# Early products with U in full single precision, more of them, and more gathered rows ahead of the dense stage

## The chip, the cores and the metric

One program on one core of one Trainium2 chip. The metric is the device time of one launch in microseconds (us); the time before is the median of three runs.

## The reference, cut to what matters

The program computes one layer for 512 prompt tokens and 32 sample tokens: retention, sparse attention, a gated sum of both, a layer norm, then PEER (product-key experts) and a last layer norm. The change lies in PEER:

```python
def block(xb):
    q = (xb @ wq).reshape(T, PEER_HEADS, PEER_DKEY).astype(jnp.float32)
    s1 = jnp.einsum('thd,hnd->thn', q[..., :half], subkeys[:, 0].astype(jnp.float32))
    s2 = jnp.einsum('thd,hnd->thn', q[..., half:], subkeys[:, 1].astype(jnp.float32))
    v1, i1 = lax.top_k(s1, PEER_TOPK)
    v2, i2 = lax.top_k(s2, PEER_TOPK)
    ...
    sc, sel = lax.top_k(cand, PEER_TOPK)
    eidx = jnp.take_along_axis(cidx, sel, axis=-1)
    g = jax.nn.softmax(sc, axis=-1)
    act = jax.nn.gelu(jnp.einsum('td,thkd->thk', xb.astype(jnp.float32), u[eidx].astype(jnp.float32)), approximate=False)
    return jnp.einsum('thk,thkd->td', g * act, v[eidx].astype(jnp.float32)).astype(x.dtype)
```

There are 16384 experts, each a row of U and a row of V of 1024 numbers; every token takes 16 of them for each of 8 heads.

## The kernel before, in words

PEER is done in two ways. For three tiles of 128 prompt tokens (DENSE, tiles 1 to 3) the kernel computes the products with **all** experts on TensorE and multiplies by gates that are zero for the experts not chosen. U and V come in 128 pieces of 128 experts (512 KB each). For the first prompt tile and the sample tokens (GATHER, tiles 0 and 4) it fetches the chosen rows one by one: a step fetches, for all 128 tokens of a tile, one row of U or V each (`rows`, L1303, an indirect DMA that GpSimd issues), and VectorE makes the dot product (L1316, `junk`) or adds the scaled row (L1322, `acc`). There are 320 such steps; they run anywhere after the choice of the gathered tiles.

The order of the program from the first layer norm on:

1. `first_norm` (L1061): normed rows are turned by TensorE and kept as two float32r parts, `x1h` and `x1l`.
2. `keys` (L1083): queries on TensorE, the 16 best keys on VectorE.
3. `choose` for GATHER (L1187, VectorE) beside `embedding` (L1139, TensorE).
4. `choose` for DENSE (L1187, VectorE): ends with `pick`, the chosen keys and gates.
5. `gate_tables` (L1259): 48 steps of 8 tokens. GpSimd makes `o2` (L1273), VectorE `o1` (L1275) and `o2` (L1277), both named `o` in the profile, TensorE multiplies them (L1282), ScalarE copies the result (L1283), which goes to DRAM as `gd`. Its first instruction on TensorE turns `pick` (L1264).
6. The dense stage (L1506): for each piece j, `u_phase(j)` (L1442) makes the activations of 384 tokens (product with U, gelu), and four pieces later `v_parts` and `v_product` (L1467, L1481) multiply by the gates and add the product with V into six PSUM tiles.
7. The last layer norms.

A product in float32r goes three times over the array (`mm3`, L157), because each operand is split in a high and a low part. The split of a weight piece (`weights`, L149, with `split`, L125) is a copy on ScalarE (`wh`, L126) and a subtraction (`wl`, L127) on VectorE, or on GpSimd. A piece of U takes 8 x 3 matmuls of 384 columns, a piece of V 6 x 3 of 512 columns.

Stages 1 to 5 are **filled** with work of the dense stage and with gathered rows. `u_early` (L938) makes the product of the next piece of U ahead of time. Before the gate tables its result goes to DRAM (`early`, `act_d`) and comes back in the dense stage (`gl`, L1448, then a gelu, L1449); the first KEPT ones made in the gate tables stay in SBUF (`kept`). `tick` (L953) decides: each step of a stage states what it costs TensorE, VectorE and ScalarE, and pieces are added until TensorE's account is as full as the others'. Rows are added in proportion to TensorE's account (RATE). The accounts are constants of the program (CF for `choose`, GY for `gate_tables`):

```python
while fill["pe"] < max(fill["dve"], fill["act"]) and fill["u"] < EARLY:
    u_early()
    fill["pe"] += 3.9
    fill["dve"] += 1.1 if UPOOL == 1 else 0.0
    fill["act"] += 1.4
```

EARLY is only a ceiling. As the program is built, 45 pieces are made early before (25 through DRAM, 20 kept), and 83 stay in the dense stage; 74 of the 320 row steps come ahead of it. With UPOOL = 2 the split of every other early piece is done by GpSimd.

Of the kernel before, what the change touches and what calls it, by code (L numbers as in the profile page):

```python
# [20 lines left out]
NT = 544  # L21
# [20 lines left out]
KEPT = 22  # L42
VR = 3
EARLY = 72
UPOOL = 2
# [4 lines left out]
CF = 0.85  # L50
# [9 lines left out]
GY = (1.8, 2.3, 1.2)  # L60
# [18 lines left out]
def tile_hybrid_step(ctx: ExitStack, tc: tile.TileContext, io):  # L79
# [24 lines left out]
    def moments(pieces, p0, p1, name):  # L104
        """1/sqrt(var + EPS) and -mean/sqrt(var + EPS) of the rows of [p, <= 512] views; the root by Newton's steps."""
# [23 lines left out]
    # ---------------------------------------------------------------- pools of the front  # L129
# [19 lines left out]
    def weights(src, n=1024, eng=V, raw=None, keep=None):  # L149
        """A [128, n] piece of a weight as its two float32r parts."""  # L150
# [26 lines left out]
    def project(chunk, evac):  # L177
        """Columns of a 128-wide chunk of W_in, transposed: [128, tokens]."""
# [8 lines left out]
    def project_nat(pieces, width, hook=lambda u: None, part=None):  # L187
        """Columns of W_in as they come: five tiles [128 tokens, columns]; pieces: (source, number of k), for width
        columns after the other. part: a tile for the sample group's four sums, each in 32 columns of the array (four
        k a piece); the fifth tile is then that group's alone."""  # L190
# [31 lines left out]
    def gates(n, tile_of):  # L222
        """Gates of the branches: the next chunks, as tanh(x / 2), to DRAM."""
# [6 lines left out]
    # ---------------------------------------------------------------- attention keys, indexer  # L230
# [29 lines left out]
    # places of the pages  # L260
# [17 lines left out]
    for i, t0 in enumerate(TILES):  # L278
# [3 lines left out]
        # keys of the attention, rotated  # L282
# [12 lines left out]
        # indexer keys: layer norm, rotated  # L295
# [43 lines left out]
    def rope_swap(dst, raw, cs, sn, blk, u, eng):  # L339
        """Rotation of rows in a chunk whose heads are blocks of 2*blk rows; sn has the source rows' signs."""  # L340
# [11 lines left out]
    # ---------------------------------------------------------------- queries of the attention  # L352
# [20 lines left out]
    # ---------------------------------------------------------------- indexer of the prompt  # L373
# [37 lines left out]
    # ---------------------------------------------------------------- indexer of the sample group  # L411
    # rows 32 q + 4 b + t: the q-th quarter of the past of token t of sequence b, then (q = 3) the new keys
# [64 lines left out]
    # the TOPK-th largest of each row, bit by bit; y = +-x so that it is not negative  # L477
# [453 lines left out]
    def u_dots(h, l):  # L931
        p = pst()
        for k in range(8):
            ks = slice(k * 128, (k + 1) * 128)
            mm3(p[:, :DT], h[:, ks], l[:, ks], x1h[:, k, D0:D0 + DT], x1l[:, k, D0:D0 + DT], k == 0, k == 7)
# [729 lines left out]
```

## Time and profile before

| | |
|---|---|
| median of 3 runs | 2661.93 us (2655.82 to 2664.12) |
| span of the profiled execution | 2726.3 us; the page gives no time of that execution besides its span |
| TensorE busy | 2478.5 us, 91% |
| VectorE busy | 1934.1 us, 71% |
| ScalarE, GpSimd busy | 35%, 36% |
| HBM traffic | 205 GB/s over the span |

Shares over the whole span mix stages with different limits, so the stages have to be looked at one by one. Names in the profile: PE is TensorE, PEld its weight loads, DVE VectorE, ACT ScalarE, POOL GpSimd. Starts of matmuls are measured, their ends are modelled and overlap the next start, so the tempo of matmuls is read from start to start. A matmul of two float32 operands is recorded twice. A granted clock of 1.00 is 2.4 GHz, the lower level is 1.2 GHz; what stands between is a mean over time at both.

### The profile page before, as it was taken

The numbers are of one execution on the slowest core, as the hardware profiler recorded it, in microseconds if no ns is written. First come the engines' busy times: TensorE is split into PE (matmuls) and PEld (weight loads), VectorE is DVE, ScalarE is ACT, GpSimd is POOL, SyncE is SP. The second block draws the span as 40 slices with busy tenths as digits, with TensorE's granted clock in tenths as the row PEclk, the third lists the DMA queues.
The fourth block names the chain that finished last, engine by engine and source line by source line (L and its number), as shares of the span: only waits on it lengthen the run. The fifth ranks groups of instructions, "written<-read, shape, count | busy, mean of one in ns | idle before, by whom it ended". The sixth has DMA issues, their size and how long they took to land.

```text
span 2726.3 us, 40425 instructions
## 1 busy us (share of the span) xinstructions
PE 2478.5 (91%) x15162; PEld 2164.6 (79%) x15162; DVE 1934.1 (71%) x3867; ACT 953.4 (35%) x1657; POOL 993.5 (36%) x773
## 2 busy tenths in 40 slices
PE   8789999999988999999887777789999999999996
PEld 8768988888655569889777766778988988888885
DVE  6685667755322245578999999977777877877777
ACT  3232333333232333243222354543333333333332
POOL 4530000001134412110356778833444444443442
PEclk9889999999998999999998998899999999999998
DMA  6322243545675554232256566579888888998883
GB/s 204 106 85 92 71 167 113 195 127 191 226 227 156 152 173 160 96 138 72 93 184 203 201 224 223 206 259 349 294 317 310 315 321 306 332 319 308 300 314 126
DMA packets 233013, 562.71 MB, mean 206 GB/s; under 512 B 26576, under 2 KB 96400, under 8 KB 230896
## 3 DMA queue, kind: packets, MB, share of 16 engines
q1 hardware_dynamic: 140576, 287.83, 31.2%
q0 software_dynamic: 58368, 205.55, 21.6%
q10 hardware_dynamic: 33872, 66.73, 6.6%
q8 instruction: 119, 1.95, 0.3%
q14 instruction: 78, 0.64, 0.1%
HBM read 491.08 MB, written 68.95 MB: 205 GB/s over the span
## 4 chain that ended last, share of the span: by engine, by line
PE 65%; DVE 19%; issue 5%; DMA 4%; another core or an unknown queue 2%; ACT 2%; POOL 1%; SPq 0%; ACTq 0%; DVEq 0%; POOLq 0%
PE ps L160 7%; PE ps L158 7%; PE ps L159 7%; PE po L159 6%; PE po L158 6%; PE po L160 6%; PE act L158 4%; PE act L159 4%; PE act L160 4%; DVE o L1277 2%; DVE junk L1316 2%; PE nat L158 2%; PE nat L160 2%; DVE acc L1322 2%
## 5 line engine op out<-in xcount | busy, mean ns | idle before, releaser
L126 ACT ACTIVATE wh<-wraw 128x1024 fp32r<-128x1024 f32 (+2 forms) x265 | 278.7, 1052 | 606.3 <-PE ps L159 207.8
L127 DVE TENSOR_TENSOR wl<-wraw,wh 128x1024 fp32r<-128x1024 f32 (+2 forms) x239 | 306.0, 1280 | 172.7 <-ACT wh L126 150.1
L1303 POOL DMA_INDIRECT rows<-u_rows,eidx x160 | 240.3, 1502 | 317.8 <-DVE junk L1316 254.4
L1303 POOL DMA_INDIRECT rows<-v_rows,eidx x160 | 240.9, 1505 | 278.9 <-DVE acc L1322 192.5
L159 PE MATMUL po<-vl,ah 128*128 128x512 f32 x768 | 301.5, 393 | 6.6 <-DVE vl L127 6.6
L158 PE MATMUL po<-vh,ah 128*128 128x512 f32 x768 | 299.7, 392 | 1.1 <-ACT vh L126 1.1
L160 PE MATMUL po<-vh,al 128*128 128x512 f32 x768 | 300.1, 391 | 0.0
L158 PE MATMUL ps<-xh,wh 128*128 128x272 f32 x960 | 284.6, 296 | 9.3 <-issue 7.7
L159 PE MATMUL ps<-xl,wh 128*128 128x272 f32 x960 | 281.8, 294 | 8.1 <-issue 8.1
L160 PE MATMUL ps<-xh,wl 128*128 128x272 f32 x960 | 283.1, 295 | 5.9 <-issue 5.9
L160 PE MATMUL ps<-x1h,wl 128*128 128x384 f32 (+1 forms) x616 | 205.2, 333 | 28.4 <-DVE wl L127 16.8
L1322 DVE SCALAR_TENSOR_TENSOR acc<-rows,co,acc 128x1024 f32<-128x1024 f32 x160 | 227.1, 1420 | 4.4 <-DMA rows<-v_rows,eidx 3.8
L158 PE MATMUL act<-x1h,wh 128*128 128x384 f32 x664 | 225.2, 339 | 1.3 <-ACT gl L1456 1.3
L159 PE MATMUL act<-x1l,wh 128*128 128x384 f32 x664 | 223.3, 336 | 0.0
L160 PE MATMUL act<-x1h,wl 128*128 128x384 f32 x664 | 223.2, 336 | 0.0
L1316 DVE SCALAR_TENSOR_TENSOR junk<-rows,x1n 128x1024 bf16<-128x1024 f32 x160 | 212.7, 1329 | 5.8 <-DMA rows<-u_rows,eidx 5.3
L158 PE MATMUL ps<-x1h,wh 128*128 128x384 f32 (+1 forms) x616 | 206.4, 335 | 11.0 <-ACT pph L1179 8.0
L159 PE MATMUL ps<-x1l,wh 128*128 128x384 f32 (+1 forms) x616 | 202.7, 329 | 0.3 <-DVE x1l L1081 0.3
L158 PEld LDWEIGHTS ps<-xh,wh 128*128 128x128 f32 x960 | 185.6, 193 | 21.2 <-issue 13.9
L821 POOL DMA_INDIRECT kv<-ckv,idp x128 | 123.3, 963 | 211.2 <-PE nat L862 153.7
L159 PEld LDWEIGHTS ps<-xl,wh 128*128 128x128 f32 x960 | 185.8, 194 | 11.4 <-issue 10.6
L160 PEld LDWEIGHTS ps<-xh,wl 128*128 128x128 f32 x960 | 185.4, 193 | 8.1 <-issue 7.5
(448 smaller groups left out, 6121.5 us busy)
## 6 DMA issues: line engine op xcount, KB each, us to landing
wraw<-u_t SPq DMA_DIRECT2D x128, 512.0 KB
vr<-v_rows SPq DMA_DIRECT2D x128, 512.0 KB
wraw<-w_t SPq DMA_DIRECT2D x60, 512.0 KB
gg<-gd SPq DMA_DIRECT2D x33, 768.0 KB
gd<-stg ACTq DMA_DIRECT2D x12, 2048.0 KB
state<-state_ret SPq DMA_DIRECT2D x32, 512.0 KB
ret_sample<-state ACTq DMA_DIRECT2D x32, 512.0 KB
wraw<-w_rv SPq DMA_DIRECT2D x16, 512.0 KB
```

The source lines that it names most:

```text
L126: S.activation(h, x, AF.Copy)
L127: eng.tensor_tensor(l, x, r32(h), op=OP.subtract)
L158: T.matmul(out, lh, rh, start=first, stop=False)
L159: T.matmul(out, lh, rl, start=False, stop=False)
L160: T.matmul(out, ll, rh, start=False, stop=last)
L821: G.indirect_dma_start(out=kv[-1][:, i, :], out_offset=None, in_=io["ckv"], in_offset=bass.IndirectOffsetOnAxis(ap=idp[:, c:c + 1], axis=0))
L1277: V.scalar_tensor_tensor(o2, o2, 0.0, pkT[:, 2, tok, None].to_broadcast([128, 8, 128]), op0=OP.is_equal, op1=OP.mult)
L1303: G.indirect_dma_start(out=r, out_offset=None, in_=io[kind + "_rows"], in_offset=bass.IndirectOffsetOnAxis(ap=idx[:, p:p + 1], axis=0))
L1316: i = V.scalar_tensor_tensor(junk, r, 1.0, x, op0=OP.mult, op1=OP.mult, accum_out=dots[:, p % 16:p % 16 + 1])
L1322: i = V.scalar_tensor_tensor(acc, r, co[:, p % 16:p % 16 + 1], acc, op0=OP.mult, op1=OP.add)
```

## The change

`u_early` no longer splits its piece of U. It multiplies the raw piece in float32 by `x1f`, a third copy of the normed rows that `first_norm` now keeps (six more ScalarE copies). So a piece is 8 float32 matmuls and no split. Raw pieces have buffers of their own until the gate tables (two, then three), where they take the six buffers of the split weights. The accounts follow: a piece counts 5.15 for TensorE and 0.5 for ScalarE, a row 1.4 for VectorE, CF grows from 0.85 to 1.5 and GY's parts for VectorE and ScalarE to 3.5 and 2.1, so that `tick` adds more pieces, and with TensorE's account more rows. KEPT falls from 22 to 18.

```diff
-KEPT = 22
+KEPT = 18
...
-EARLY = 72
-UPOOL = 2
+EARLY = 96
...
-CF = 0.85
+CF = 1.5
...
-GY = (1.8, 2.3, 1.2)
+GY = (1.8, 3.5, 2.1)
...
-    def u_dots(h, l):
+    def u_early():
+        j = fill["u"]
+        fill["u"] = j + 1
+        if "u" in epool:
+            raw = epool["u"].tile([128, 1024], F32, name="uraw")
+        else:
+            raw = wst.tile([128, 1024], F32, name="uraw", tag=("wh", "wl", "wraw")[j % 3])
+        load(raw, io["u_t"][j])
         p = pst()
         for k in range(8):
-            ks = slice(k * 128, (k + 1) * 128)
-            mm3(p[:, :DT], h[:, ks], l[:, ks], x1h[:, k, D0:D0 + DT], x1l[:, k, D0:D0 + DT], k == 0, k == 7)
-        return p
-    def u_early():
-        j = fill["u"]
-        fill["u"] = j + 1
-        p = u_dots(*weights(io["u_t"][j], eng=G if j % UPOOL else V))
+            T.matmul(p[:, :DT], raw[:, k * 128:(k + 1) * 128], x1f[:, k], start=k == 0, stop=k == 7)
...
             u_early()
-            fill["pe"] += 3.9
-            fill["dve"] += 1.1 if UPOOL == 1 else 0.0
-            fill["act"] += 1.4
+            fill["pe"] += 5.15
+            fill["act"] += 0.5
...
-            fill["dve"] += 1.15
+            fill["dve"] += 1.4
...
+                if t in DENSE:
+                    S.activation(x1f[:, k:k + 4, c0 - D0:c0 - D0 + n], pt[:, :, :n], AF.Copy)
...
+    x1f = pers.tile([128, 8, DT], F32, name="x1f")
...
-    deque(first_norm(pc, FIRST[1], between), 0)
+    with ExitStack() as us:
+        epool["u"] = pool(us, "u0", 2, side="right")
+        deque(first_norm(pool(us, "l1", side="right"), FIRST[1], between), 0)
+    epool["u"] = pool(hps, "u1", 3, side="right")
...
+        del epool["u"]
         run(gate_tables(gb))
```

What `tick` makes of it, counted in the built programs:

| | before | changed |
|---|---|---|
| early pieces of U: start of the keys / end of the keys to the gate tables / gate tables | 2 / 23 / 20 | 2 / 33 / 39 |
| of these through DRAM / kept | 25 / 20 | 56 / 18 |
| pieces of U in the dense stage | 83 | 54 |
| row steps before the gate tables / in them / in the dense stage | 26 / 48 / 246 | 49 / 84 / 187 |
| splits of U on VectorE / GpSimd from the end of the keys through the gate tables | 25 / 21 | 3 / 0 (three of VectorE's are of dense pieces, before and now) |

On TensorE at the end of the embedding (`ph`, `wh`), before the gate tables begin (`pick`). Before, the first and the last of the pieces of U that stand there; each float32r matmul is a row of its own, 528 of them in all, that is 22 pieces:

```order
L158 MATMUL ps<-x1h,wh 128x384
L159 MATMUL ps<-x1l,wh 128x384
L160 MATMUL ps<-x1h,wl 128x384
L158 MATMUL ps<-x1h,wh 128x384
L159 MATMUL ps<-x1l,wh 128x384
L160 MATMUL ps<-x1h,wl 128x384
L1264 MATMUL ps<-ident,pick_11314 128x128 x3
```

And in the changed program, with the first steps of the gate tables (`o`):

```order
L157 MATMUL ps<-wh,ph 128x256
L158 MATMUL ps<-wl,ph 128x256
L159 MATMUL ps<-wh,pl 128x256
L941 MATMUL ps<-x1f,uraw 128x384 x256
L1265 MATMUL ps<-ident,pick_11315 128x128 x3
L941 MATMUL ps<-x1f,uraw 128x384 x5
L1283 MATMUL nat<-o_15706,o_15705 128x128 x8
L941 MATMUL ps<-x1f,uraw 128x384 x4
L1283 MATMUL nat<-o_15741,o_15740 128x128 x8
L941 MATMUL ps<-x1f,uraw 128x384 x7
L1283 MATMUL nat<-o_15776,o_15775 128x128 x8
```

Between the embedding and the gate tables now stand 256 float32 matmuls, 32 pieces, where 22 stood; in the gate tables a whole piece stands between most steps.

On VectorE at the start of the gate tables (`acc` is a gathered row). Before:

```order
L1275 TENSOR_TENSOR o_15973<-iota,pkT 128x1024
L1277 SCALAR_TENSOR_TENSOR o_15974<-o_15974,pkT 128x1024
L1275 TENSOR_TENSOR o_15990<-iota,pkT 128x1024
L1277 SCALAR_TENSOR_TENSOR o_15991<-o_15991,pkT 128x1024
L1322 SCALAR_TENSOR_TENSOR acc_14827<-rows,co,acc_14827 128x1024
L1275 TENSOR_TENSOR o_16010<-iota,pkT 128x1024
L1277 SCALAR_TENSOR_TENSOR o_16011<-o_16011,pkT 128x1024
L1322 SCALAR_TENSOR_TENSOR acc_14827<-rows,co,acc_14827 128x1024
```

And now:

```order
L1276 TENSOR_TENSOR o_15705<-iota,pkT 128x1024
L1278 SCALAR_TENSOR_TENSOR o_15706<-o_15706,pkT 128x1024
L1323 SCALAR_TENSOR_TENSOR acc_14765<-rows,co,acc_14765 128x1024
L1276 TENSOR_TENSOR o_15740<-iota,pkT 128x1024
L1323 SCALAR_TENSOR_TENSOR acc_14765<-rows,co,acc_14765 128x1024
L1278 SCALAR_TENSOR_TENSOR o_15741<-o_15741,pkT 128x1024
L1323 SCALAR_TENSOR_TENSOR acc_14765<-rows,co,acc_14765 128x1024
L1276 TENSOR_TENSOR o_15775<-iota,pkT 128x1024
```

A row stands now after nearly every instruction of the gate tables, about one and three quarters for each pair of `o`, where one stood.

## Rows read from the trace of the kernel before

**Rows 1.** Busy time by stage: keys, choices with embedding, choice of DENSE, gate tables, dense
```profile
core 0: us, PE busy (x) PEld busy (x) DVE busy (x) ACT busy (x) POOL busy (x), PEclk, DMA share, GB/s
1185.00:1312.00 127.00, 127.00 (x986) 121.34 (x985) 99.73 (x556) 45.22 (x130) 2.39 (x1) 1.00 0.21 71
1312.00:1399.00 87.00, 68.10 (x525) 59.98 (x523) 83.35 (x306) 23.08 (x53) 37.82 (x20) 0.92 0.35 119
1399.00:1528.00 129.00, 105.26 (x524) 101.09 (x525) 122.82 (x282) 35.91 (x53) 79.71 (x44) 0.91 0.66 220
1528.00:1813.00 285.00, 209.42 (x1277) 198.17 (x1277) 279.47 (x183) 137.18 (x163) 222.44 (x106) 0.89 0.60 212
1813.00:2690.00 877.00, 868.23 (x4240) 772.44 (x4239) 660.23 (x846) 314.54 (x450) 358.23 (x242) 1.00 0.87 311
```

**Rows 2.** All waits of PE in the dense stage: us in total, times, longest
```profile
PE po L159 <- DVE vl L127: 6.4, 4, 3.4
PE act L158 <- ACT gl L1456: 1.3, 1, 1.3
PE po L158 <- ACT vh L126: 1.1, 1, 1.1
```

**Rows 3.** PE in order of time, dense stage: a piece of U, then one of V
```profile
2061.64 0.34 PE L159 MATMUL act<-x1l,wh 128*128 128x384 f32 x1
...
2064.45 0.34 PE L160 MATMUL act<-x1h,wl 128*128 128x384 f32 x1
2064.63 0.39 PE L158 MATMUL po<-vh,ah 128*128 128x512 f32 x1
...
2071.00 0.39 PE L159 MATMUL po<-vl,ah 128*128 128x512 f32 x1
```

**Rows 4.** Float32 matmuls: by tile (ns min/median/max, first and last start), and in order of time
```profile
L1465 PE MATMUL po<-vr,ident x12: 590/593/594, 2462.2 to 2466.9; 128*128 128x512 f32 x12
```
```profile
1575.65 1.95 PE L1282 MATMUL nat<-o,o 128*128 128x128 f32 x16
```

**Rows 5.** The first piece of U after the embedding, and the turning of `pick`
```profile
1398.88 0.69 PE L158 MATMUL ps<-x1h,wh 128*128 128x384 f32 x1 [8.03 <-ACT pph L1179]
```
```profile
L1264 PE MATMUL ps<-ident,pick x9: 271/272/421, 1528.9 to 1715.1; 128*128 128x128 f32 x9
```

**Rows 6.** ACT in order of time in the first layer norm
```profile
1162.66 1.55 ACT L1078 ACTIVATE x1h<-ps 128x512 fp32r<-128x512 f32 x3
```

**Rows 7.** Groups of DVE and POOL, 1399 to 1528: count, busy us, mean ns, idle before
```profile
L1316 DVE SCALAR_TENSOR_TENSOR junk<-rows,x1n 128x1024 bf16<-128x1024 f32 x14 | 16.9, 1210 | 0.0
L127 DVE TENSOR_TENSOR wl<-wraw,wh 128x1024 fp32r<-128x1024 f32 x11 | 16.8, 1526 | 2.0 <-ACT wh L126 2.0
```
```profile
L127 POOL TENSOR_TENSOR wl<-wraw,wh 128x1024 fp32r<-128x1024 f32 x11 | 31.5, 2860 | 9.4 <-ACT wh L126 9.3
```

**Rows 8.** Gathered rows by tile, 1399 to 1528: ns min/median/max, first and last start
```profile
L1303 POOL DMA_INDIRECT rows<-v_rows,eidx x14: 932/950/4238, 1460.1 to 1524.3; - x14
...
L1322 DVE SCALAR_TENSOR_TENSOR acc<-rows,co,acc x10: 1271/1276/2280, 1479.7 to 1522.7; 128x1024 f32<-128x1024 f32 x10
```

**Rows 9.** Groups of DVE, gate tables, 1528 to 1813
```profile
L1275 DVE TENSOR_TENSOR o<-iota,pkT 128x1024 f32<-128x1024 f32 x48 | 89.3, 1860 | 0.0
L1277 DVE SCALAR_TENSOR_TENSOR o<-o,pkT 128x1024 f32<-128x1024 f32 x48 | 80.0, 1666 | 0.0
L1316 DVE SCALAR_TENSOR_TENSOR junk<-rows,x1n 128x1024 bf16<-128x1024 f32 x26 | 49.5, 1903 | 0.0
L1322 DVE SCALAR_TENSOR_TENSOR acc<-rows,co,acc 128x1024 f32<-128x1024 f32 x22 | 48.7, 2212 | 0.0
L127 DVE TENSOR_TENSOR wl<-wraw,wh 128x1024 fp32r<-128x1024 f32 x12 | 23.5, 1961 | 7.8 <-ACT wh L126 7.8
```

**Rows 10.** Groups of POOL, gate tables, 1528 to 1813
```profile
L1273 POOL TENSOR_TENSOR o<-iota,pkT 128x1024 f32<-128x1024 f32 x48 | 112.1, 2339 | 12.5 <-PE nat L1282 9.3 <-ACT pkT L1266 2.5
L1303 POOL DMA_INDIRECT rows<-u_rows,eidx x30 | 51.2, 1708 | 31.4 <-DVE junk L1316 24.0 <-DVE acc L1322 6.1 <-issue 1.2
L1303 POOL DMA_INDIRECT rows<-v_rows,eidx x18 | 31.5, 1751 | 12.4 <-DVE acc L1322 9.1 <-issue 1.4 <-DVE junk L1316 1.4
L127 POOL TENSOR_TENSOR wl<-wraw,wh 128x1024 fp32r<-128x1024 f32 x10 | 30.1, 3014 | 1.8 <-ACT wh L126 1.8
```

**Rows 11.** ACT in the dense stage: its waits for activations loaded back
```profile
ACT gl L1449 <- DMA gl<-act_d: 101.9, 23, 8.1
```

**Rows 12.** Waits of ACT for raw pieces of U, 1399 to 1529
```profile
ACT wh L126 <- DMA wraw<-u_t: 22.5, 5, 5.3
```

**Rows 13.** DMA of the dense stage
```profile
DMA packets 120643, 272.65 MB, mean 311 GB/s; under 512 B 8242, under 2 KB 62130, under 8 KB 120458
```

More of the change, by code (lines that the diff above doesn't have):

```diff
@@ L929, in tile_hybrid_step @@
     fill = {"pe": 0.0, "dve": 0.0, "act": 0.0, "n": 0, "rate": 0.0, "gat": None, "u": 0}
-    def u_dots(h, l):
-        p = pst()
-        for k in range(8):
-            ks = slice(k * 128, (k + 1) * 128)
-            mm3(p[:, :DT], h[:, ks], l[:, ks], x1h[:, k, D0:D0 + DT], x1l[:, k, D0:D0 + DT], k == 0, k == 7)
-        return p
     def u_early():
@@ L940, in u_early @@
         fill["u"] = j + 1
-        p = u_dots(*weights(io["u_t"][j], eng=G if j % UPOOL else V))
+        if "u" in epool:
[3 more added lines that the diff above has]
+        load(raw, io["u_t"][j])
+        p = pst()
+        for k in range(8):
+            T.matmul(p[:, :DT], raw[:, k * 128:(k + 1) * 128], x1f[:, k], start=k == 0, stop=k == 7)
         if "kept" in epool and len(kept) < KEPT:
@@ L1143, in embedding @@
         for k in range(2):
-            raw = pw.tile([128, NT], F32, name="praw", bufs=1)
+            raw = wst.tile([128, 1024], F32, name="wraw")[:, :NT]
             load(raw, io["pT"][k])
@@ L1198, in choose @@
         se = pw.tile([128, nh, 16], U32, name="se")
-        cf = pw.tile([128, nh, 64], F32, name="cand")
+        cf = pw.tile([128, nh, 64], F32, name="cand", bufs=1)
         for s0, a0, na, nb in ((0, 0, 1, 16), (16, 1, 3, 8), (40, 4, 4, 4), (56, 8, 8, 1)):
```

## The prediction

> **What bounds the kernel now.** I read the busy time by stage first, because the shares of the whole span hide that two engines take turns. In the dense stage TensorE is busy 868 of 877 us at a granted clock of 1.00, so at 2.4 GHz; VectorE is busy 75%. In the choice of DENSE and in the gate tables it is the other way round: VectorE is busy 123 of 129 and 279 of 285 us, TensorE only 105 and 209, at a mean granted clock of 0.91 and 0.89, so part of the time at 1.2 GHz [rows 1]. The waits agree: in the dense stage TensorE waits 8.8 us in all [rows 2]. So a piece of U taken out of the dense stage gives back its full TensorE time there, and what it costs earlier depends on who ends last in the stage that takes it in.
>
> The tempo of matmuls comes from their starts. A float32r matmul of 384 columns comes every (2064.45 - 2061.64) / 16 = 0.176 us, one of 512 every (2071.00 - 2064.63) / 28 = 0.228 us [rows 3]. So a piece of U costs 24 x 0.176 = 4.2 us, a piece of V 18 x 0.228 = 4.1 us, and 83 and 128 of them make 350 + 524 = 874 us: the dense stage is explained by these two alone. A float32 matmul is two records. With 512 columns a record comes every (2466.9 - 2462.2) / 11 = 0.427 us, with 128 columns every (1.95 - 0.27) / 15 = 0.112 us [rows 4] (the last of a burst is taken off at the 0.27 us that one record lasts [rows 5]). None has 384 columns: scaled down from 512 a record takes 0.320 us, scaled up from 128 it takes 0.336. I take 0.320, the nearer row, and 16 x 0.320 = 5.1 us for a piece. So an early piece becomes dearer for TensorE by 0.9 us; what it sheds is the split.
>
> **The change part by part.** All sums are against the profiled execution, span 2726.3 us; the median of the runs is 2661.9, 0.976 of it, and the result is scaled by that.
>
> *Start, 1157 to 1185, and the end of the keys.* Six more ScalarE copies of 128x512, 1.55 / 3 = 0.5 us each [rows 6], hold PSUM buffers that the turning needs: 0 if covered, 3 us if not. Three pieces there cost 0.9 us more each on a TensorE that is 100% busy in the keys [rows 1]. I take +4 (0 to +6).
>
> *From the embedding to the gate tables.* Before, the first piece of U started at 1398.9 and `pick` was turned at 1528.9 [rows 5]: 130 us, set by VectorE. In the changed order 32 pieces stand on TensorE between the embedding and that turning: 32 x 5.1 = 164 us. VectorE's side: 23 more rows at 1.25 us (1.21 and 1.28 [rows 7, 8]) are +29; 11 splits fewer are -13; and 11 GpSimd splits fewer [rows 7] free it of blocking, worked out below as 1.74 us each, -19. Its account so stays where it was, -3, and TensorE ends last: +34. A gain is excluded, since all 32 pieces stand ahead of the turning in one queue. The upper bound is the same work at this stage's clock of 0.91, 180 us: +50. I take +34, because a TensorE that no longer waits for splits runs on without pauses. VectorE has only a row or two to do ahead of its first `o`, so the 34 us are idle time there.
>
> *Gate tables, 285 us.* VectorE's 1024-wide operations take 1.21 us alone, but 1.67 to 2.21 here [rows 9]. The excess is 53 us on the 96 `o`, 39 on the 48 rows, 9 on the 12 splits: 101 us, over the 58 tensor operations of GpSimd beside them [rows 10], 1.74 us each. So GpSimd's work blocks VectorE, and the 48 that make `o` stay. Added: 36 rows x 1.25 = 45 us; removed: 9 splits x 1.21 = 11 and 10 GpSimd splits x 1.74 = 17. VectorE: 285 + 17 = 302 us. If new rows paid the blocked mean of 2.05 us, it would be +57; below the 17, every bit of blocking that a GpSimd operation could cause is 3.0 us, its own length [rows 10]. TensorE: 39 pieces x 5.1 = 200, and 768 records x 0.112 = 86, together 286 us at 2.4 GHz, 321 at the present 0.89. The two engines, bound to each other every step, are now nearly equal, so neither bound is met: I take the middle between 302 and 321, 312, +27 (+1 to +57).
>
> The Trainium skill (SBUF — State Buffer, section "SBUF: two separate sides") says that VectorE and GpSimd share a port pair as an exclusive lock for the whole instruction. By that rule a removed GpSimd split of 3.0 us would give VectorE back 3.0 us, not 1.74, and the stage would be 13 us shorter on VectorE's side; the mean here is smaller, so the trace bears out the blocking but not its full length.
>
> *Dense stage.* 29 pieces fewer: 29 x 4.2 = -122 us. VectorE loses 29 splits and 59 rows, 660 - 110 = 550 of some 766 us. DMA moved 273 MB at 311 GB/s [rows 13]; 29 pieces and 59 rows of 0.52 MB fewer and 31 loads of 0.2 MB more leave 233 MB, 304 GB/s. So neither is nearer to its limit. What grows is the loads of `act_d`: 56 for 25. ScalarE waited for them 101.9 us, 23 times [rows 11], with the splits of V queued behind it, but TensorE waited 8.8 us in all [rows 2]. Nothing is late below zero; above, all 31 new loads at 101.9 / 23 = 4.4 us would be 137 us. I take the waits of TensorE in proportion, 8.8 x 56 / 25 = 20, so +11, as they were well hidden. Net -111.
>
> Sum: 4 + 34 + 27 - 111 = -46, scaled -45: 2661.9 - 45 = **2617 us**.
>
> **Rivals.**
>
> *A, faster: the gate tables don't grow.* VectorE gets back all of the 30 us of GpSimd's splits (289 us), TensorE without pauses runs at 2.4 GHz (286 us), and the loads of `act_d` stay hidden: 4 + 34 + 4 - 122 = -80, 2584 us. For it: TensorE's clock in the dense stage is 1.00 as soon as it isn't paused. Against it: two engines in step lose something. Chance 0.17.
>
> *B, GpSimd becomes the bound of the gate tables.* An indirect DMA takes GpSimd 0.95 us in the choice [rows 8], but 1.7 us in the gate tables beside VectorE's long operations [rows 10]. If each of 84 waited out a whole row operation, 0.95 + 1.21 = 2.16 us, GpSimd needs 112 + 181 us and, with its present 44 us of waits for rows to come free, 337 us: +52 in place of +27, 2642 us. Against it: 82.7 us for 48 is 1.7 each, not 2.16. Chance 0.15. The same page of the Trainium skill, SBUF — State Buffer, warns in that section that GpSimd cannot write descriptors while VectorE holds the shared ports; the longer fetches agree with it, if not at full length.
>
> *C, slower: loads of `act_d` reach TensorE.* ScalarE takes its work in order, so a gelu that waits for its load delays the split of the next V. With more early pieces in a row there is less time per piece: 4.1 us where an early piece follows an early one. If all 31 new loads cost TensorE the 4.4 us that ScalarE waits, the sum without my 11 turns from -57 to +80: 2740 us. It decides from 57 / 31 = 1.8 us a load. Against it: 25 loads made TensorE wait 8.8 us at most. Chance 0.07.
>
> *D, slower: raw pieces come late.* TensorE now takes pieces straight from the load. In the choice ScalarE waited 22.5 us, 5 times, for 21 pieces or so [rows 12]: 1.07 us a piece. For 71 pieces that is 76 us, and 2661.9 + 29 = 2691. Against it: three or six buffers where there were two. Chance 0.05.
>
> That the change doesn't do what it says can be left out for the counts, which the built order fixes; it can only fail in the 0.320 us, and at 0.336 it would cost 71 x 0.26 = 18 us, within the range.
>
> **How the numbers follow.** The forecast has 0.53; its own range, from the bounds of the choice (+34 to +50) and of the gate tables (TensorE's 286 or VectorE's 302 to 321), is 2600 to 2648. A has 0.17, B 0.15, C 0.07, D 0.05, and 0.03 is left for none of them, around no change. The range 2580 to 2660 takes in the forecast, B and nearly all of A, and leaves out C, D and a part of the rest, under 2 in 10. A measurement of this kernel tells some 0.3%, 8 us, from no change. Faster by more: most of the forecast, A and most of B, 0.80; within it: the upper ends of the forecast and B and what is left over, 0.08; slower: C and D, 0.12.
>
> **What would show it.** In the changed profile `uraw` records should start every 0.32 us; 32 pieces should run almost without a pause from about 1403 to 1567, with VectorE idle some 30 us ahead of its first `o`; the gate tables should last about 312 us with TensorE's clock above 0.89 and no GpSimd splits; the dense stage some 766 us with TensorE waiting about 20 us. The prediction is wrong if the choice of DENSE isn't ended by TensorE, if the gate tables pass 340 us (B), or if TensorE waits over 60 us in the dense stage (C).

## The result and the profile after

The changed kernel is **slower**, by 1.8%: 2711.1 us median (2703.8 to 2714.1) against 2660.3 (2655.8 to 2664.1) for the kernel before on the same chip, ratio 1.018 (95% interval 1.017 to 1.020). The forecast was 2617, range 2580 to 2660.

The code ahead of the keys hardly differs, but its length did from one profile to the next: the first matmul of the keys started between 1137.5 and 1222.9 us in fourteen profiles, and the changed kernel's first profile has 1137.5 where that of before has 1194.4. So I count stages from marks behind it, each read from one tile's first or last start on TensorE: K, the first matmul with `skT`; T, the first of the gate tables (`nat<-o,o`); G, the last of those; E, the end of the span.

| us | K to T (keys, choices, embedding) | T to G (tables) | G to E (dense, last norms) | K to E |
|---|---|---|---|---|
| before | 342.6 | 273.5 | 915.8 | 1531.9 |
| changed | 394.8 | 317.8 | 862.2 | 1574.8 |
| difference | +52 | +44 | -54 | +43 |
| forecast | +34 | +27 | -111 | -50 |

(The +4 of the forecast lies ahead of K, but for one piece's 0.9 us.) Every term has the sign of the forecast, and every one fell on the bad side of its size. A second profile of the changed kernel (run 12) has the same 1574.8 us in all, but single stages differ by 2, 5 and 7 us: a smaller difference than that between two stages says nothing. Busy time by stage of the changed kernel, in the columns of [rows 1]:

```profile
1137.00:1255.00 118.00, 118.00 (x899) 110.22 (x898) 99.19 (x559) 43.50 (x127) 2.35 (x1) 1.00 0.22 72
1255.00:1342.00 87.00, 71.57 (x535) 63.02 (x534) 83.47 (x311) 22.61 (x54) 38.99 (x23) 0.91 0.48 164
1342.00:1525.00 183.00, 171.43 (x512) 99.87 (x511) 115.72 (x303) 20.72 (x41) 72.79 (x52) 0.95 0.73 246
1525.00:1856.00 331.00, 304.64 (x1402) 214.44 (x1400) 269.63 (x221) 125.27 (x161) 236.74 (x132) 0.95 0.77 275
1856.00:2680.00 824.00, 778.97 (x3574) 666.36 (x3575) 560.45 (x733) 285.67 (x425) 281.87 (x184) 0.97 0.80 282
```

The keys stayed as they were. In the choice of DENSE the two engines changed places: TensorE is busy 171 of 183 us, VectorE 116. In the gate tables TensorE now leads with 305 of 331 us, VectorE has 270. The dense stage is where the profile departs most from [rows 1]: TensorE is busy 779 of 824 us at a granted clock of 0.97, where it was 868 of 877 at 1.00.

Its waits in the dense stage (us in total, times, longest), 45 us where [rows 2] had 8.8:

```profile
PE po L157 <- ACT ah L125: 22.9, 10, 3.4
PE po L158 <- DVE vl L126: 11.9, 18, 1.5
PE po L157 <- ACT vh L125: 8.8, 4, 3.7
PE act L157 <- ACT gl L1462: 1.1, 1, 1.1
PE act L157 <- ACT early L947: 0.6, 1, 0.6
```

All large ones are for the splits of V and of the activations, first of all those that ScalarE makes (`ah`, `vh`). And ScalarE's own wait, the row that answers to [rows 11]:

```profile
ACT gl L1455 <- DMA gl<-act_d: 243.6, 39, 9.9
```

6.2 us each, 39 times, where it was 4.4, 23 times. ScalarE and SP's queue in order of time, with one line of VectorE, 13 us of that stage, show how one such wait comes about:

```profile
2331.28 0.53 ACT L125 ACTIVATE ah<-gl 128x384 fp32r<-128x384 f32 x1 [5.34 <-PE po L158]
2331.71 1.05 ACT L125 ACTIVATE vh<-vr 128x1024 fp32r<-128x1024 f32 x1
...
2333.46 1.22 DVE L126 TENSOR_TENSOR vl<-vr,vh 128x1024 fp32r<-128x1024 f32 x1
...
2334.70 0.33 SPq L1428 DMA_DIRECT2D vr<-v_rows  x1
2335.08 0.43 SPq L1454 DMA_DIRECT2D gl<-act_d  x1
2335.55 1.06 ACT L125 ACTIVATE wh<-wraw 128x1024 fp32r<-128x1024 f32 x1 [1.76 <-PE act L158]
2336.51 0.47 ACT L1462 ACTIVATE gl<-act 128x384 f32<-128x384 f32 x1
...
2343.81 0.53 ACT L1455 ACTIVATE gl<-gl 128x384 f32<-128x384 f32 x1 [6.83 <-DMA gl<-act_d]
```

ScalarE splits a piece of V (`vh`, 2331.71). That, with VectorE's half of the split (`vl`, until 2334.68), frees a buffer `vr`, and SP issues the next load of V. Only behind it, in the same queue, goes the load of `act_d`, at 2335.08. ScalarE is through with its other work at 2336.98 and stands for 6.8 us, a piece and a half of TensorE's time, with the next `ah` and `vh` queued behind. In this stage such a load lands 4.4 to 9.3 us after its issue (median 6.1, this one 8.7); this one was issued 1.9 us before ScalarE had nothing else to do.

In the order of the built program this is the rule: 47 of the 56 loads stand on SP's queue behind the load of V that waits for the very split that ScalarE does just ahead of their gelu (in the kernel before, 19 of 25).

The DMA traffic of the dense stage, beside [rows 13], fell as forecast (233 MB), so there was not more to transfer:

```profile
DMA packets 112569, 232.08 MB, mean 282 GB/s; under 512 B 7345, under 2 KB 65329, under 8 KB 112440
```

In the choice and the tables, the tempo of the float32 pieces, one unbroken burst of TensorE:

```profile
1399.62 24.67 PE L941 MATMUL ps<-x1f,uraw 128*128 128x384 f32 x76
```

From start to start that is (24.67 - 0.49) / 75 = 0.322 us a record, with the modelled 0.49 us of the last one taken off: 5.16 us a piece, where the estimate from 512 columns was 5.1. TensorE's waits from the end of the keys to the dense stage are no longer for raw data or U's splits:

```profile
PE nat L1283 <- DVE o L1278: 25.7, 13, 4.6
PE ps L941 <- ACT early L947: 11.6, 2, 7.9
PE nat L158 <- DVE wl L126: 5.4, 2, 3.0
PE ps L941 <- ACT pph L1180: 5.1, 1, 5.1
```

The second of these, 11.6 us ahead of pieces of U, has the same root as the waits of the dense stage. ScalarE stood 22 us for VectorE's `pick`, and later 16 us for a row's dot product, with the copy that frees TensorE's PSUM buffer next in line:

```profile
1434.01 0.31 ACT L1236 ACTIVATE pick<-pick 128x128 f32<-128x128 f32 x1 [22.08 <-DVE pick L1235]
1434.22 0.47 ACT L947 ACTIVATE early<-ps 128x384 f32<-128x384 f32 x1
```

VectorE's groups and waits in the tables answer to [rows 9], GpSimd's to [rows 10]:

```profile
L1278 DVE SCALAR_TENSOR_TENSOR o<-o,pkT 128x1024 f32<-128x1024 f32 x48 | 87.7, 1828 | 31.8 <-POOL o L1274 31.8
L1323 DVE SCALAR_TENSOR_TENSOR acc<-rows,co,acc 128x1024 f32<-128x1024 f32 x47 | 74.3, 1580 | 7.6 <-DMA rows<-v_rows,eidx 7.4
L1276 DVE TENSOR_TENSOR o<-iota,pkT 128x1024 f32<-128x1024 f32 x48 | 65.0, 1356 | 68.3 <-ACT pkT L1267 68.3
L1317 DVE SCALAR_TENSOR_TENSOR junk<-rows,x1n 128x1024 bf16<-128x1024 f32 x37 | 51.4, 1389 | 3.9 <-DMA rows<-u_rows,eidx 3.7
```
```profile
L1274 POOL TENSOR_TENSOR o<-iota,pkT 128x1024 f32<-128x1024 f32 x48 | 106.7, 2232 | 69.4 <-ACT pkT L1267 66.5 <-PE nat L1283 2.3
L1304 POOL DMA_INDIRECT rows<-v_rows,eidx x43 | 66.5, 1547 | 31.2 <-DVE acc L1323 24.4 <-issue 2.4 <-DVE junk L1317 1.9
```

VectorE's work got cheaper (an `o` pair 3.18 us for 3.53, the rows 1.4 and 1.6 for 1.9 and 2.2), but VectorE stood idle for 68 us for `pkT`, 58 of them ahead of its first `o`: the turning of `pick` stands on TensorE behind the 32 pieces.

### The profile page after: what moved, and what is told of

Same layout as the page of the kernel before. It is cut to its first block, busy times and chain, and to the rows that moved or that the text cites. A ratio compares the mean times of both kernels' runs of the same rounds, so it can differ in the third digit from the quotient of the medians.

```text
span 2712.3 us, 39128 instructions
## 1 busy us (share of the span) xinstructions
PE 2536.1 (94%) x14570; PEld 2056.4 (76%) x14570; DVE 1811.8 (67%) x3815; ACT 893.2 (33%) x1618; POOL 930.0 (34%) x751
## 4 chain that ended last, share of the span: by engine, by line
PE 55%; DVE 17%; DMA 12%; issue 8%; POOL 5%; ACT 2%; SPq 0%; DVEq 0%; ACTq 0%; POOLq 0%
PE ps L157 6%; PE ps L159 6%; PE ps L158 6%; DMA gl<-act_d 6%; PE po L158 4%; PE po L159 4%; PE po L157 4%; PE ps L941 3%; PE nat L157 2%; PE nat L840 2%; PE nat L159 2%; PE nat L158 2%; DVE acc L1323 2%; DVE junk L1317 2%; DVE vl L126 2%
## 5 line engine op out<-in xcount | busy, mean ns | idle before, releaser
L941 PE MATMUL ps<-x1f,uraw 128*128 128x384 f32 x1184 | 404.5, 500 | 16.7 <-ACT early L947 11.6
L941 PEld LDWEIGHTS ps<-x1f,uraw 128*128 128x128 f32 x1184 | 228.8, 197 | 169.2 <-issue 12.9
L157 PE MATMUL po<-vh,ah 128*128 128x512 f32 x768 | 307.9, 403 | 31.8 <-ACT ah L125 22.9
L125 ACT ACTIVATE wh<-wraw 128x1024 fp32r<-128x1024 f32 (+1 forms) x191 | 200.1, 1048 | 396.3 <-PE ps L158 163.3
L126 DVE TENSOR_TENSOR wl<-wraw,wh 128x1024 fp32r<-128x1024 f32 (+2 forms) x187 | 229.9, 1229 | 120.3 <-ACT wh L125 107.3
L1317 DVE SCALAR_TENSOR_TENSOR junk<-rows,x1n 128x1024 bf16<-128x1024 f32 x160 | 201.4, 1259 | 14.0 <-DMA rows<-u_rows,eidx 13.3
L157 PEld LDWEIGHTS po<-vh,ah 128*128 128x128 f32 x768 | 149.1, 194 | 68.6 <-ACT ah L125 27.3
L158 PEld LDWEIGHTS po<-vl,ah 128*128 128x128 f32 x768 | 148.3, 193 | 48.8 <-DVE vl L126 19.4
L159 PEld LDWEIGHTS po<-vh,al 128*128 128x128 f32 x768 | 148.5, 193 | 34.2 <-DVE al L126 3.0
L1480 DVE TENSOR_TENSOR gl<-gl,gg 128x384 f32<-128x384 f32 x110 | 59.8, 553 | 157.2 <-ACT gl L1455 154.0
```

The costliest lines, as they stand in the source:

```text
L125: S.activation(h, x, AF.Copy)
L126: eng.tensor_tensor(l, x, r32(h), op=OP.subtract)
L157: T.matmul(out, lh, rh, start=first, stop=False)
L158: T.matmul(out, lh, rl, start=False, stop=False)
L159: T.matmul(out, ll, rh, start=False, stop=last)
L941: T.matmul(p[:, :DT], raw[:, k * 128:(k + 1) * 128], x1f[:, k], start=k == 0, stop=k == 7)
```

## The experiments

Three theories. **1**: the loads of `act_d` are issued too late, ScalarE waits for them in order, and TensorE waits and slows; besides, more pieces and rows were taken ahead than the early stages hold. **2**: the dense stage is short of something else (DMA, VectorE), and the loads are hidden as before. **3**: the float32 product itself is the loss. Stage lengths in the text are K to T, T to G and G to E unless a stretch is given. The expectations use other marks, the first `pick` and the first `act`, which lie 7 to 9 us ahead of T and from 3 us ahead of G to 6 behind it, in all kernels but `half_pieces`.

**1. Without the loads.** The gelu reads other data, and the 56 loads of `act_d` are left out.

```diff
-            load(gl, act_d[j])
-            S.activation(gl, gl, AF.Gelu)
+            S.activation(gl, x1f[:, 0], AF.Gelu)
```

> The changed kernel, but the 56 activations that went through DRAM aren't loaded back: the gelu reads a tile that is on chip anyway (left out: 56 loads of 192 KB, and their values). Theory 1 (in the dense stage the loads back are late, ScalarE waits for them in order, and TensorE then waits and drops to its lower clock): the dense stage falls from 824 to about 775 us, TensorE's waits from 45 us to under 15, the granted clock rises to 0.99 or 1.00, and the time falls from 2711 by 40 to 50 us to 2661 to 2671 us. Theory 2 (the dense stage is short of DMA or of something else, and the loads back are hidden): less than 10 us faster, 2701 us or more.

Measured: 397.2, 319.0, **793.0**; ratio 0.995 (0.991 to 0.9998). Busy time of its dense stage, and all of TensorE's waits there:

```profile
1908.00:2665.00 757.00, 751.39 (x3579) 656.23 (x3580) 565.81 (x736) 291.10 (x427) 277.29 (x184) 1.00 0.83 292
```
```profile
PE po L157 <- ACT vh L125: 4.5, 1, 4.5
PE po L158 <- DVE vl L126: 0.7, 1, 0.7
PE act L157 <- ACT early L947: 0.6, 1, 0.6
```

The loads cost 862 - 793 = 69 us, 1.2 us each and more than the 40 to 50 expected: some 39 us of waits and, for the same matmuls, 779 - 751 = 28 us that TensorE was busy longer at the clock of 0.97. Without them the dense stage is 123 us shorter than before, near the forecast's 122. So the loads are not hidden, and theory 2 falls in that. Whether it is their order or the transfers themselves that cost the time, run 3 tells.

**2. The loads emitted five pieces earlier**, with as many more buffers (and KEPT 14 to make room).

```diff
-KEPT = 18
+KEPT = 14
+BACK = 5
...
+            fetch_back(n + BACK)
             j = order[n]
             aa[j] = u_phase(j)
```

> The changed kernel with the loads of act_d issued five pieces earlier (ten buffers of gl in place of five, for which KEPT falls from 18 to 14). Theory 1: ScalarE finds nearly all of them landed, its wait for them falls from 244 us to under 80, TensorE's waits in the dense stage from 45 us to under 25; 25 to 45 us faster than the changed kernel, 2666 to 2686 us. Theory 2: within 8 us of 2711.

Measured: 397.4, 316.1, 861.8; ratio 1.023 (1.016 to 1.030). No change, and ScalarE waits as before:

```profile
ACT gl L1455 <- DMA gl<-act_d: 261.2, 42, 10.7
```

At first sight this speaks against theory 1. But the built order shows that the edit did not reach its aim: the scheduler places instructions by its own reckoning, and 49 of 60 loads stood again behind the load of V that waits for the split just ahead. The source was written earlier; the queue was not.

**3. The same loads, the gelu pinned later.** This time the order is forced on ScalarE: the gelu of a reloaded activation is issued behind the V split of its own piece.

```diff
             load(gl, act_d[j])
-            S.activation(gl, gl, AF.Gelu)
...
-        split(h, l, raw)
+        ga["v"] = split(h, l, raw)
...
+        if j < early and j not in kept:
+            with tc.issue_after(ga["v"].ins):
+                S.activation(gl, gl, AF.Gelu)
```

> The changed kernel with one order altered: the gelu of a reloaded activation stands on ScalarE behind the V split of its own piece, so that, counted in the built order, its load is issued one to two V splits before it is wanted and not behind the V load that waits for the split just ahead of it. Nothing is left out and no load fewer. Theory 1 (the loads are issued too late, ScalarE waits for each in order): ScalarE's waits for act_d fall from 244 us to under 60, TensorE's waits in the dense stage from 45 us to under 15, the dense stage from 856 us to 785 to 805, ratio to the kernel before 0.99 to 1.01. Theory 2 (the transfers themselves take the place of others, whatever their order): the dense stage stays within 10 us of 856, ratio 1.015 to 1.025. Both: the other stages stay at 388 and 331 us.

Measured: 397.1, 319.8, **801.6**; ratio 0.996 (0.993 to 0.9998). ScalarE no longer waits for `act_d` at all; its first two waits in the dense stage, then TensorE's:

```profile
ACT ah L125 <- PE po L159: 141.2, 62, 7.6
ACT vh L125 <- PE po L160: 113.8, 49, 4.1
```
```profile
PE po L158 <- ACT ah L125: 6.4, 3, 3.7
PE po L159 <- DVE vl L126: 3.7, 2, 3.1
PE act L158 <- ACT early L948: 0.6, 1, 0.6
```

ScalarE now waits for TensorE, as it should. The same 56 transfers, ordered otherwise, give back 61 of the 69 us, and the slower kernel is now as fast as the one before, if anything slightly faster. Theory 1 holds for the dense stage.

**4. The control: the kernel before with the same pinning.**

> The kernel before (split pieces, its own accounts) with the order of pin_gelu for its 25 reloaded activations. If the loads cost the kernel before as little as its TensorE waits say (8.8 us in the dense stage, of 25 loads), the dense stage falls from 916 us to 905 to 914, the rest stays, ratio 0.993 to 1.000, and the gain of balanced (0.9815) comes from float32 pieces and their place. If the order alone is what makes balanced fast: ratio 0.98 to 0.985, the dense stage under 890 us.

Measured: 342.7, 275.5, 910.4; ratio 0.999 (0.995 to 1.004). 25 loads cost the kernel before about 5 us, 0.2 us each, which is no more than the scatter of this stage. So the pinning alone makes nothing faster where few loads stand. And the price of a load is not a constant: 31 more of them cost some 64 us, 2.1 us each.

**5. Split pieces in the same places.** The kernel before with the changed accounts, KEPT and EARLY, so the same 74 pieces and 133 rows ahead, but split into float32r parts.

> The kernel before with the changed accounts (CF, GY, row cost, EARLY, KEPT, and 5.15 and 0.5 for a piece), so that the same 74 pieces and 133 rows come early in the same stages as in the changed kernel, but with splits and three float32r matmuls. Theory 1 (too many pieces and rows are taken ahead for either method; float32 only moves the bound from VectorE to TensorE): about 2720 us (2705 to 2740); from the embedding to the gate tables some 167 us in place of 183, gate tables some 359 in place of 331, both ended by VectorE. Theory 3 (float32 on TensorE is itself the loss, the number of pieces is right): 2680 us or less, as TensorE then needs 134 us for 32 pieces instead of 164.

Measured: 398.1, **364.8**, 871.6; ratio 1.038 (1.030 to 1.046). From the keys on it takes 1634.5 us against 1574.8: float32 pieces are worth 60 us at the same places, 47 of them in the tables. Theory 3 falls. The kernel is slower than theory 1 had it too (1.038 for about 1.02), and the choice did not become 16 us shorter with the cheaper products, but stayed as it was.

**6. Float32 pieces with the accounts of before** (CF 0.85, GY 1.8, 2.3, 1.2, a row 1.15): 35 pieces and 74 rows ahead.

> The changed kernel with the accounts of before for the stages (CF 0.85, GY 1.8, 2.3, 1.2, row 1.15): float32 pieces, but only 35 of them early and 74 rows, as before. Theory 1: VectorE is relieved of splits and of blocking and is not loaded again; from the embedding to the gate tables about 100 us in place of 130 before, gate tables about 257 in place of 285, the dense stage 42 us longer for 10 more pieces: about 2643 us (2630 to 2655), faster than before. Theory 3: no faster than before, 2655 us or more.

Measured: 305.1, 243.9, 958.0, so 1507.0 from the keys on, 25 us less than before; ratio 1.001 (0.998 to 1.005). The two early stages beat the kernel before by 37 and 30 us. The timed ratio does not show it; the part ahead of the keys was 22 us longer in its profile than in that of before, and why is open.

**7. Half the rows.** Every second row that the accounts call for is left to the dense stage; the pieces stay.

```diff
-            if next(fill["gat"], None) is None:
+            if (fill["rate"] != RATE or fill["n"] % 2 == 0) and next(fill["gat"], None) is None:
```

> The changed kernel, but every second gathered row that the accounts call for ahead of the dense stage is left to the dense stage: 67 rows ahead in place of 133, the same 74 pieces of U. Theory P (the choice and the gate tables go at the pace of TensorE's pieces): keys to first pick stays at 388 us and first pick to dense at 331, within 8 us each. Theory V (they go at VectorE's pace): 24 rows of 1.4 us fewer and 42 fewer give 34 and 59 us, so 354 and 272. Theory G (GpSimd's instructions and VectorE's shut each other out in the gate tables): only the second falls, by 30 us or more. The dense stage takes 66 rows more: under 10 us if they lie beside TensorE's work, up to 90 if not.

Measured: 379.4, 293.0, 916.7; ratio 1.023 (1.017 to 1.030).

**8. Half the pieces**, all the rows.

```diff
-            u_early()
+            fill["c"] = fill.get("c", 0) + 1
+            if fill["c"] % 2:
+                u_early()
```

> The changed kernel, but every second piece of U that the accounts call for ahead of the dense stage is left to the dense stage: 38 pieces ahead in place of 74, the same 133 rows. Theory P: 16 pieces of 5.1 us fewer take up to 80 us from 388, down to VectorE's pace of some 340, and 21 fewer take up to 107 from 331, down to VectorE's 270 to 290. Theory V: both stay within 8 us. Both: the dense stage has 36 pieces of 4.2 us more, 151 us, and 36 loads of act_d fewer, so with what the loads cost now, 69 us for 56, 856 + 151 - 44 = 963 us.

Measured: 331.6, 287.5, 944.8; ratio 1.011 (1.004 to 1.018). (Its first `pick` and first `act` both come before the stage ahead of them has ended, so here only K, T, G and E can be used.) The tables from T to G in the changed kernel, with half the rows, and with half the pieces:

```profile
1532.00:1850.00 318.00, 295.22 (x1371) 209.33 (x1372) 265.31 (x219) 122.08 (x157) 230.22 (x130) 0.95 0.78 280
```
```profile
1575.00:1868.00 293.00, 284.29 (x1372) 203.01 (x1373) 201.30 (x157) 122.05 (x157) 162.02 (x88) 0.98 0.65 232
```
```profile
1543.00:1830.00 287.00, 206.91 (x1037) 159.71 (x1037) 280.44 (x214) 113.71 (x134) 240.25 (x129) 0.88 0.71 254
```

With half the rows TensorE bounds the tables (284 of 293 us, VectorE 201); with half the pieces VectorE does (280 of 287, TensorE 207). With both in full neither is met, and the stage is 25 and 30 us longer. So theory P and theory V are each half right: the changed accounts load both engines at once, and what two engines in step then lose goes on top. In the choice the pieces matter most: 14 fewer ahead of T give 63 us, 24 rows fewer 15 us. GpSimd, busy 230 of 318 us, bounds nothing.

The dense stage of `half_rows` took 54 us more for 66 rows. Is that a price of the rows? TensorE's waits there:

```profile
PE po L157 <- ACT ah L125: 42.4, 11, 6.4
PE po L158 <- DVE vl L126: 19.0, 20, 2.8
PE po L157 <- ACT vh L125: 17.6, 9, 3.5
```

**9. Half the rows, with the pinned order.**

> half_rows with the order of pin_gelu. In half_rows the 66 rows more took the dense stage from 856 to 911 us; the question is whether rows have a price there of their own. Theory R (rows lie beside TensorE's work, and cost only because VectorE is later still for a ScalarE that already waits for late loads): the dense stage takes 795 to 810 us, as in pin_gelu (795.5). Theory S (a row in the dense stage costs 0.8 us in itself, 66 rows 54 us): 845 to 855 us. Keys to dense 678 us as in half_rows in both.

Measured: 378.9, 293.0, **813.6**; ratio 0.988 (0.985 to 0.991). The stage falls by 103 us, and the 66 rows cost 12 against `pin_gelu`. Rows lie beside TensorE's work once ScalarE is no longer late. That they otherwise lengthen VectorE's part of the same chain is the likely reason for the 54 us, but not shown by a run of its own.

**10. Balanced.** The pinned order and fewer of both ahead: CF 1.2, a row 1.25, RATE 1 / 7.0; 45 pieces, 44 rows.

> The order of pin_gelu, and fewer rows and pieces ahead: CF 1.2 and 1.25 us for a row in place of 1.5 and 1.4, and a rate of rows of 1/7 in place of 1/3.4; 45 pieces and 44 rows come ahead in place of 74 and 133. If rows in the dense stage lie beside TensorE's work and the reloads no longer hold ScalarE: keys to dense 510 to 550 us as in f32_old_accounts (546 with 35 pieces and 74 rows), the dense stage 757 + 29 x 4.2 + 30 = 909 us, 1420 to 1460 us from the keys to the end against 1532 before and 1575 in the changed kernel, ratio 0.96 to 0.98. If the 59 rows more do delay the dense stage: 1480 to 1520 us, ratio 0.985 to 1.00.

Measured: 312.9, 237.5, 914.7, together 1465.1; **2679.9 us against 2735.5, ratio 0.981 (0.976 to 0.987)**: faster than both kernels, if a little less than the first of the two ranges. Its tables and its dense stage:

```profile
1521.00:1758.00 237.00, 212.55 (x1114) 160.04 (x1112) 208.53 (x141) 113.42 (x139) 151.68 (x76) 0.94 0.58 207
1758.00:2600.00 842.00, 837.74 (x4097) 745.12 (x4096) 670.59 (x863) 310.01 (x440) 389.62 (x264) 1.00 0.93 333
```

It makes as many pieces early as the kernel before and has the same dense stage (914.7 for 915.8); the gain lies ahead of it, 30 us in the choice and 36 in the tables, from pieces without splits and 30 rows fewer. How much each of the two gives is not shown, as no run has split pieces with 44 rows. In these tables the engines are as even as in the changed kernel, and lose as much: TensorE is busy 213 and VectorE 209 of 237 us, 24 us more than the longer one, where `half_rows` lost 9 and `half_pieces` 7. The stage is shorter because there is less in it, not because one engine has room.

**11. Fewer still** (CF 1.0, RATE 1 / 10; 38 pieces, 27 rows).

> balanced with CF 1.0 and a rate of 1/10: 38 pieces and 27 rows ahead in place of 45 and 44. If TensorE bounds every stage of balanced, moving a piece back costs 4.2 us in the dense stage and gives back 5.1 ahead of it: keys to dense 555 - 36 = 520 us, the dense stage 910 + 29 = 939, together 1459 against 1465, ratio 0.976 to 0.984 to the kernel before. If the 17 rows more in the dense stage (its DMA share is 0.93 in balanced) have a price there: dense 950 us or more, ratio 0.985 to 0.99.

Measured: 296.3, 233.3, 943.6, together 1473.2; ratio 0.984 (0.977 to 0.992). Moving seven pieces and 17 rows back gives 21 us and costs 29, so going on in this direction does not pay. Whether something between `balanced` and the changed kernel is faster still was not tried.

**12. The changed kernel again**, on the chip of runs 4, 9 and 11.

> The changed kernel once more, on the chip of these runs, as the measure for the stage lengths: 388, 331 and 856 us within 5, ratio 1.015 to 1.025 by all theories; the part ahead of the keys may be longer than the 1138 us of its first profile, as it was in every other one (1186 to 1217).

Measured: 397.1, 322.7, 855.0, together 1574.8 as in its first profile; ratio 1.022 (1.014 to 1.030). What differs is the part ahead of the keys, 1222.4 us for 1137.5.

## Why the prediction was wrong

*Dense stage: forecast -111, measured -54. This is the step that failed*: "I take the waits of TensorE in proportion, 8.8 x 56 / 25 = 20, so +11, as they were well hidden." The 29 pieces gave about their 122 us (123 without any loads, of which some 5 belong to the loads of the kernel before). But the loads cost 64 us more than before, not 11: TensorE waited 45 us, not 20, and was busy 28 us longer. The mechanism was named, as rival C, down to its price: it decides from 1.8 us a load, and a new load cost 2.1. I gave it 0.07, on the ground that 25 loads had cost TensorE 8.8 us. The likely reason that the proportion failed: a wait that is hidden because other work lies between two of them does not grow in proportion when that work is taken away. In the kernel before 83 late pieces, each with 4.2 us of TensorE's time for the product with U, stood among 25 loads; now 54 among 56. No run changes only this. What points to it are other kernels without the pinning: with 20 loads among 90 and 93 late pieces (`half_pieces`, `f32_old_accounts`) TensorE waited 10 and 12 us in the dense stage, with 56 among 54 (`splits_same_pieces`) 51. [Rows 11] held the warning, 23 waits in 25 loads, since it says that nearly every load was late already and only the queue of ready work behind ScalarE hid it. What I priced at nothing besides was TensorE's own tempo at the lower clock, some 20 of the 28 us that it was busy longer.

*From the embedding to the tables: forecast +34, measured +52.* The place was right: 32 pieces of 5.16 us stand ahead of the turning, TensorE sets the end, and VectorE waits ahead of its first `o`, 58 us. That "a TensorE that no longer waits for splits runs on without pauses" is the part that failed: it waited 12 us for ScalarE's copies `early` and ran at a mean clock of 0.95, 14 of the 183 us at 1.2 GHz. (The 5 us for `pph` lie ahead of the first piece, where the kernel before had 8.) My upper bound, +50, took the clock into account and not the waits.

*Gate tables: forecast +27, measured +44 (+46 from `pick` to the first `act`, the marks of the forecast).* That is the top of my bounds as they should have been. The +57 leaves out the 11 us of the nine splits; with them it is +46. TensorE's own time was right: 286 us at full clock, 284 with half the rows at 0.98. VectorE's 302 came out somewhat lower, 280 with half the pieces. I took the middle between VectorE's 302 and TensorE's 321; two engines in step lost 25 us on top of what the longer one alone took.

That GpSimd blocks VectorE is borne out: the excess over the unblocked 1.21 us (1.28 for `acc`), 7 us on the first `o`, 30 on the second, 14 and 7 on the rows, is 58 us for GpSimd's 48 tensor operations, 1.2 us each where it was 1.74. But I misread these means as a block of less than full length. VectorE's 1024-wide operations take 1.2 to 1.3 us or, when they are long, mostly 2.9, with little between:

```profile
1580.95 2.06 POOL L1274 TENSOR_TENSOR o<-iota,pkT 128x1024 f32<-128x1024 f32 x1
1581.19 2.90 DVE L1276 TENSOR_TENSOR o<-iota,pkT 128x1024 f32<-128x1024 f32 x1
...
1586.30 1.21 DVE L1276 TENSOR_TENSOR o<-iota,pkT 128x1024 f32<-128x1024 f32 x1
```

GpSimd's operation ends at 1583.01, and the one that VectorE started 0.24 us after it ends 1.08 us later. So do 32 of the 34 long ones of this stage, and all 57 in the tables of the kernel before. The Trainium skill (SBUF — State Buffer, "SBUF: two separate sides") has whichever of the two starts first hold the shared ports for the whole instruction; the rows agree. The mean is smaller than GpSimd's 2.2 us because VectorE's operation starts a little later, and because GpSimd made 48 where 32 of VectorE's had to wait, as VectorE now stood idle for part of them. So 1.74 us was the right price for a removed split, and not a sign of a partial block.

*Float32 at 384 columns*: estimate 0.320 us a record, measured 0.322. Right.

*Rivals.* A (tables don't grow, loads hidden) failed in both halves. B: GpSimd was busy 230 of 318 us and its fetches took 1.55 us, not 2.16; not the bound. Its mechanism is in the trace all the same. A fetch takes 0.94 us with VectorE idle, and one that starts while a wide operation of VectorE runs ends some 0.8 us behind the end of that operation:

```profile
1576.58 1.21 DVE L1276 TENSOR_TENSOR o<-iota,pkT 128x1024 f32<-128x1024 f32 x1
1576.93 1.68 POOL L1304 DMA_INDIRECT rows<-u_rows,eidx  x1 [0.64 <-DVE acc L1323]
```

The Trainium skill (SBUF — State Buffer, "SBUF: two separate sides"), which B names for this, says it of VectorE's two-port modes; the rows show it for operations with two inputs from SBUF.

D: no wait of TensorE for a raw piece shows; three and six buffers were enough. C came true at about half of its price (2.1 us a load, not 4.4), together with two terms that were each 17 or 18 us short. The three misses, 57 + 18 + 17 = 92 us, are the distance from -50 to +43.

*The range and the signs.* The forecast's own range, 2600 to 2648, does not follow from the bounds that it names: they give 2592 (with VectorE's 302 for the tables 2607) to 2641. That changes nothing here, as the result lies outside both. None of the three signs of being wrong came up (the choice was ended by TensorE, the tables took 331 us, TensorE waited 45 us in the dense stage), and yet the forecast was wrong. The sign for C counted TensorE's waits alone, and not the time that it lost at the lower clock.

## What to carry to other kernels

Before taking more work ahead through DRAM, look where its reload stands in its queue, not at how long the transfer takes: a load behind another that waits for a buffer is issued when that buffer comes free, and an engine that works in order then stands for the full landing time. A hidden wait is priced by the work that hides it; if the change removes that work, a price in proportion is too low (here 11 us, where 64 were paid and 137 was the upper bound). And a filler that evens two engines' accounts has to count what they lose in step, some 25 us of a stage here: the best version took 45 pieces and 44 rows ahead, not 74 and 133.

## What was unexpected of the hardware

TensorE's pauses cost more than their length. In the dense stage of the changed kernel 45 us of waits, none over 3.7 us, came with a granted clock of 0.97 and 28 us more busy time for the same matmuls, against 1.00 without the loads. The trace's record of the clock has eleven stretches at 1.2 GHz there, 44 us in all, though TensorE was busy 95% of the stage. Each begins in a pause of 1.5 to 3.7 us or at most 2.4 us behind its end; one of the twelve pauses of that length has none. One of them, in the columns time, busy us, clock, DMA share and GB/s:

```profile
2422.00:2425.00 3.00, 0.04 (x1) 1.00 1.03 353
2426.00:2428.00 2.00, 2.00 (x5) 0.50 0.55 212
```

At half speed 44 us lose 22, and without the loads there were 3 us at the lower clock: so some 20 of the 28 us are the clock's.

The part ahead of the keys took 1137.5 us in one profile of the changed kernel and 1222.4 in another. In its first 200 us TensorE was busy 178 us at a granted clock of 0.97 in the one, 154 us at 0.86 in the other. It does not come from the change: the kernel before took 2660 us beside the result and 2735 to 2740 in the later sets of runs, about as much more. What sets it is open.
